# Searching 112 pair sums instead of 256, five searches placed in the query projection, and new prices in the up-projection's work list

## The chip, the cores and the metric

The kernel runs on one core of one Trainium2 chip. The metric is device time in microseconds (us) of one execution; three runs of the kernel before are given. Engine names are those of the profile: PE is TensorE (matmul), PEld its weight loads, DVE VectorE, ACT ScalarE, POOL GpSimd, SP the engine that only issues DMAs.

## What is computed

The reference is a two-layer model on 512 tokens of width 1024. Each layer ends in a PEER feed-forward block, and the change touches only that block:

```python
q = (h @ q_w).reshape(T, PEER_HEADS, 2, PEER_HALF)
s = jnp.einsum('thcd,ckd->thck', q, sub_keys)
s1, i1 = lax.top_k(s[:, :, 0], 16)          # 16 best of 128, first half
s2, i2 = lax.top_k(s[:, :, 1], 16)          # 16 best of 128, second half
cand_s = (s1[..., :, None] + s2[..., None, :]).reshape(T, 8, 256)
cand_i = (i1[..., :, None] * 128 + i2[..., None, :]).reshape(T, 8, 256)
best_s, best_pos = lax.top_k(cand_s, 16)
idx = jnp.take_along_axis(cand_i, best_pos, axis=-1)
gate = jax.nn.softmax(best_s, axis=-1)
a = jnp.einsum('nd,nhkd->nhk', hb, u[ib])   # ib: idx
w = gb * jax.nn.gelu(a, approximate=False)  # gb: gate
out = jnp.einsum('nhk,nhkd->nd', w, v[ib])
```

For each token and each of 8 heads, the 16 best of 16384 experts are found by two searches among 128 and one among the 256 sums of their results. Both lists `s1` and `s2` come out sorted, from best to worst.

## The kernel before

Tokens lie in four tiles of 128, numbered `tt` = 0 to 3. In each layer `peer` has three stages.

**Query projection** (lines 949 to 980). Sixteen chunks `c`, each 24 matmuls of 128x512 (`lin`, `mm3`, lines 200 to 214: every product is taken in three parts, high times high, high times low, low times high). The function `score` of one chunk runs after the next chunk's matmuls: it multiplies by the sub-keys (L971) and ACT copies the scores out, tiles 0 and 3 to `early` (L976, three buffers), tiles 1 and 2 to `late` (L977, which the profile calls `gv`). Chunks 2h and 2h+1 give head h. Each `score` advances the generator `bg_topk` by one step, and `bg_topk` searches a head of tiles 0 and 3 as soon as both its chunks are there, so every second step only waits. In the same chunks, `napply` (c = 3 to 10) makes the normalised activations for the next stage: a DVE operation (L760) and a copy on ACT (L764).

**Up-projection** (lines 982 to 1003). 128 chunks `j`, each 24 matmuls of 128x384 (`hhi`, `hlo`) over tiles 1 to 3; ACT makes the high part of each weight chunk (`whi`, L169) and POOL the low part in four pieces (`wlo`, L172). Tile 0 goes another way: its 128 x 16 experts are fetched row by row, by indirect DMAs that POOL issues (L695; 1.17 a chunk, `URATE`), five row buffers, and DVE multiplies each row with the activations (L678). Beside this stage runs a list of work, made in `bg` (lines 912 to 947). Each chunk adds 2.65 (`BRATE`) to a credit, an item is taken while the credit is above zero, and each takes its price off (`work`, lines 184 to 190):

```python
T: (6.0, topk of one head of one tile)
D: (0.3, decode_g) (5.0, decode_i first) (5.0, decode_i second) (0.8, decode_e)
G: (1.5, onehot for 4 tokens; its matmuls, gmm, two items later)
```

T is a search, D turns a tile's 128 winning positions into expert numbers and gates (D(0) starts the row fetches), G builds two one-hot matrices on DVE (`early` L884, `og` L886) whose product on PE (L898) spreads the gates over the experts; there are 96 G, 32 for each of tiles 1 to 3. The matrix so made goes to memory (`G`) by an ACT DMA every fourth G. The list's order is written out by hand in lines 931 to 934. Once it has ended, `load_g` reads `G` back in three parts on SP, one a chunk.

**Down-projection** (lines 1013 to 1051). 128 chunks again; the gates read back from `G` are multiplied with the first product (`GA`), and DVE, not POOL, makes `wlo`.

The change touches `topk` (L794), `decode_g`, `decode_i`, `decode_e` (L816 to L874), `bg_topk` (L904) and `bg` (L912).

Of the kernel before, what the change touches and what calls it, by code (L numbers as in the profile page):

```python
# [11 lines left out]
F32 = _mybir.dt.float32  # L12
# [50 lines left out]
class Net:  # L63
# [90 lines left out]
    def next_w(self):  # L154
# [5 lines left out]
        while self.ndma < min(len(self.srcs), i + self.LA + 1) or self.nsplit < min(len(self.srcs), i + self.SA + 1):  # L160
# [479 lines left out]
    def peer(self, L):  # L640
        nc, t, tc = self.nc, self.t, self.tc
        mm = nc.tensor.matmul
        vt = nc.vector
# [103 lines left out]
        with ExitStack() as ctx:  # L747
            mp = ctx.enter_context(tc.tile_pool(name="pm", bufs=2, reuse_waits="tile"))
# [26 lines left out]
            best = hp.tile([P, NTT, HEADS, TOPK], F32, name="best")  # L775
            pos = hp.tile([P, NTT, HEADS, TOPK], U32, name="pos")
# [17 lines left out]
            def topk(jobs):  # L794
                v = {}
                one, two = [], []
                for n, (tt, hd) in enumerate(jobs):
                    v[n] = mp.tile([P, 2, TOPK], F32, name=f"tv{n}")
                    for c in range(2):
                        src = early[hd][:, first.index(tt), c] if tt in first else late[:, later.index(tt), hd, c]  # L800
                        one.append((src, v[n][:, c, :], idx[:, c, tt, hd, :]))
                top16(one)
                for n, (tt, hd) in enumerate(jobs):
                    cand = mp.tile([P, TOPK, TOPK], F32, name=f"cand{n}", bufs=1)
                    vt.tensor_tensor(cand, v[n][:, 0, :, None].to_broadcast([P, TOPK, TOPK]),
                                     v[n][:, 1, None, :].to_broadcast([P, TOPK, TOPK]), op=OP.add)
                    two.append((cand.rearrange("p a b -> p (a b)"), best[:, tt, hd, :], pos[:, tt, hd, :]))
                top16(two)

            HK = HEADS * TOPK  # L810
            dec = {}
# [4 lines left out]
            def decode_g(tt):  # L816
                gt = mp.tile([P, HEADS, TOPK], F32, name="gt", bufs=1)
                vt.tensor_tensor(gt, best[:, tt], best[:, tt, :, 0:1].to_broadcast([P, HEADS, TOPK]), op=OP.subtract)
                dec[tt] = gt, []
                return lambda: nc.scalar.activation(gt, gt, AF.Exp, scale=self.rv[:, tt:tt + 1])  # L820

            def decode_i(tt, c):
                pi = mp.tile([P, HEADS, TOPK], U32, name="pi", bufs=1)
                if c == 0:
                    vt.tensor_single_scalar(pi, pos[:, tt], 4, op=OP.logical_shift_right)
                else:
                    vt.tensor_single_scalar(pi, pos[:, tt], 15, op=OP.bitwise_and)
                pb = mp.tile([P, TOPK, HEADS], F16, name="pb", bufs=1)
                vt.tensor_copy(pb, pi.rearrange("p h k -> p k h"))
                ib = mp.tile([P, TOPK, HEADS], F16, name="ib")  # L830
                vt.tensor_copy(ib, idx[:, c, tt].rearrange("p h a -> p a h"))
                eq = mp.tile([P, TOPK, HK], F16, name="eq", bufs=1)
                vt.tensor_tensor(eq.rearrange("p a (n q) -> p a n q", q=QT),  # L833
                                 fl(pb).rearrange("p (n q) -> p n q", q=QT)[:, None].to_broadcast([P, TOPK, HK // QT, QT]),
                                 i16[:, :, None, :].to_broadcast([P, TOPK, HK // QT, QT]), op=OP.is_equal)
                e4 = eq.rearrange("p a (k h) -> p a k h", h=HEADS)
                vt.tensor_tensor(e4, e4, ib[:, :, None, :].to_broadcast([P, TOPK, TOPK, HEADS]), op=OP.mult)  # L837
                n = TOPK // 2
                while n > 1:
                    vt.tensor_tensor(eq[:, :n], eq[:, :n], eq[:, n:2 * n], op=OP.add)  # L840
                    n //= 2
                f = mp.tile([P, HK], F32, name=f"fi{c}", bufs=1)
                vt.tensor_tensor(f, eq[:, 0], eq[:, 1], op=OP.add)
                dec[tt][1].append(f)

            def decode_e(tt):
                gt, fi = dec.pop(tt)
                sm = mp.tile([P, 2, HEADS], F32, name="sm")
                vt.tensor_reduce(sm[:, 0], gt, axis=AX.X, op=OP.add)
                vt.reciprocal(sm[:, 1], sm[:, 0])  # L850
                gk = mp.tile([P, TOPK, HEADS], F32, name="gk", bufs=1)
                vt.tensor_tensor(gk, gt.rearrange("p h k -> p k h"), sm[:, 1, None, :].to_broadcast([P, TOPK, HEADS]),
                                 op=OP.mult)
                if tt == 0:
                    ef = wg[:, 0]
                    vt.tensor_scalar(ef, fi[0], float(P), float(L * NBLK * P), op0=OP.mult, op1=OP.add)
                    vt.tensor_tensor(ef, ef, fi[1], op=OP.add)
                    vt.tensor_copy(eg, ef)
                    vt.tensor_copy(gate, fl(gk))

                def turn():
                    if tt == 0:
                        self.gi = 0
# [40 lines left out]
            def bg_topk():  # L904
                done = 0
                for hd in range(HEADS):
                    while self.hready <= hd:
                        yield
                    topk([(tt, hd) for tt in first])
                    yield  # L910

            def bg():  # L912
                items = []

                def T(tt, *hds):
                    for hd in hds:
                        items.append((6.0, lambda hd=hd: topk([(tt, hd)])))

                def D(tt):
                    items.append((0.3, lambda: decode_g(tt), 2))  # L920
                    items.append((5.0, lambda: decode_i(tt, 0)))
                    items.append((5.0, lambda: decode_i(tt, 1)))
                    items.append((0.8, lambda: decode_e(tt), 2))

                def G_(tt, lo, hi):
                    def one(b):
                        o = onehot(b)
                        return lambda: gmm(b, o)
                    for b in range(32 * tt + lo, 32 * tt + hi):
                        items.append((1.5, lambda b=b: one(b), 2))  # L930
                D(0), T(1, 0, 1), D(3), T(1, 2, 3, 4), G_(3, 0, 12), T(1, 5, 6), G_(3, 12, 20), T(1, 7), D(1)
                G_(3, 20, 28), T(2, 0), G_(3, 28, 32), T(2, 1), G_(1, 0, 4), T(2, 2), G_(1, 4, 8), T(2, 3)
                G_(1, 8, 12), T(2, 4), G_(1, 12, 16), T(2, 5), G_(1, 16, 20), T(2, 6), G_(1, 20, 22), T(2, 7), D(2)
                G_(1, 22, 32), G_(2, 0, 32)
                prev = []
                for cost, f, *late in items:
                    g = f()
                    for q in prev:
                        q[0] -= 1
                    while prev and prev[0][0] <= 0:  # L940
                        prev.pop(0)[1]()
                    if g is not None:
                        prev.append([late[0] if late else 1, g])
                    yield cost
                yield 3.0
                for _, g in prev:
                    g()
# [58 lines left out]
        with vctx:  # L1006
            mp = vctx.enter_context(tc.tile_pool(name="pv", bufs=3, reuse_waits="tile"))
# [5 lines left out]
            for j in range(NBLK):  # L1013
# [14 lines left out]
                w = self.next_w()  # L1028
# [528 lines left out]
```

## Time and profile before

| | us |
|---|---|
| median of three runs | 3432.62 (3429.08 to 3437.0) |
| profiled execution, its own time | 3430.42 |
| its span, first to last instruction | 3428.5 |
| PE busy | 3281.8 (96%) |
| DVE busy | 2712.8 (79%) |
| POOL busy | 1968.1 (57%) |
| ACT busy | 1452.7 (42%) |
| mean granted TensorE clock | 0.988 of full speed |

Busy shares are means over stages with different limits. PE's share hardly tells them apart, since matmuls overlap: what counts is how far apart successive matmuls start. The stages of the first layer's `peer` lie at 528 to 634 us (query), 634 to 1263 (up) and 1263 to 1803 (down); those of the second at 2080 to 2186, 2186 to 2816 and 2816 to 3356.

### The profile page before, as it was taken

Reading aid. Unit: us, or ns where it says so; the run is one execution under the profiler, and the core shown is the slowest. Engines: PE = TensorE matmul, PEld = TensorE weight load, DVE = VectorE, ACT = ScalarE, POOL = GpSimd, SP = SyncE. Lnnn points to the kernel's source line nnn. Section 1 sums busy time; section 2 is a strip of 40 time slices with the busy share of each in tenths; the row PEclk is TensorE's granted clock in tenths of the full one; section 3 lists DMA queues with packets and bytes.
Section 4 is the critical chain, followed back from the end, with each engine's and each line's share of the span. In section 5 each row is a group of like instructions: output and inputs, shape, how many; then the busy total and the mean of one; then the engine's idle time right before and its main releaser. Section 6 shows DMA issues by size and latency. Waiting matters only on the chain.

```text
span 3428.5 us, 52077 instructions
## 1 busy us (share of the span) xinstructions
PE 3281.8 (96%) x18814; PEld 3007.1 (88%) x18814; DVE 2712.8 (79%) x4880; ACT 1452.7 (42%) x2198; POOL 1968.1 (57%) x2168
## 2 busy tenths in 40 slices
PE   8999999998999999999998999999999999999997
PEld 5777777988999989999996668989998989999996
DVE  7667667899999748877877855899999837877775
ACT  4333334444545533333334553444445533333334
POOL 5444546799989884222216226689999994322214
PEclk9999999999999999999999999999999999999998
DMA  3222212488999989999983112488898989999982
GB/s 123 88 75 68 74 62 76 148 293 304 318 319 318 338 312 353 359 338 342 340 276 105 44 56 88 128 291 306 314 336 297 340 308 362 355 334 346 338 300 84
DMA packets 357298, 827.48 MB, mean 241 GB/s; under 512 B 30000, under 2 KB 196528, under 8 KB 350896
## 3 DMA queue, kind: packets, MB, share of 16 engines
q1 hardware_dynamic: 235136, 448.59, 40.4%
q0 software_dynamic: 73728, 268.47, 21.4%
q10 hardware_dynamic: 48176, 107.10, 8.1%
q8 instruction: 147, 2.41, 0.3%
q14 instruction: 111, 0.91, 0.1%
HBM read 717.09 MB, written 106.95 MB: 240 GB/s over the span
## 4 chain that ended last, share of the span: by engine, by line
PE 54%; DVE 32%; POOL 5%; DMA 4%; issue 3%; ACT 1%; POOLq 0%; SPq 0%; ACTq 0%; DVEq 0%
PE bank L202 16%; PE bank L203 16%; PE bank L204 16%; DVE row L678 6%; DVE early L884 6%; DVE og L886 5%; POOL wlo L172 4%; DMA row<-u,eg 2%; DVE eq L840 1%; POOL row L695 1%; DMA wraw<-v 1%; PE bank L971 1%; DVE eq L837 1%; DVE eq L833 1%; DMA wraw<-ut 1%
## 5 line engine op out<-in xcount | busy, mean ns | idle before, releaser
L172 POOL TENSOR_TENSOR wlo<-wraw,whi 128x256 fp32r<-128x256 f32 x1564 | 1279.4, 850 | 517.3 <-ACT whi L169 468.3
L169 ACT ACTIVATE whi<-wraw 128x1024 fp32r<-128x1024 f32 x647 | 685.6, 1061 | 787.8 <-issue 341.1
L695 POOL DMA_INDIRECT row<-v,eg x256 | 305.4, 1193 | 723.2 <-DVE yg L687 708.7
L204 PE MATMUL bank<-hhi,wlo 128*128 128x384 f32 x2048 | 695.1, 339 | 19.1 <-POOL wlo L172 18.7
L202 PE MATMUL bank<-hhi,whi 128*128 128x384 f32 x2048 | 703.6, 344 | 0.0
L203 PE MATMUL bank<-hlo,whi 128*128 128x384 f32 x2048 | 691.2, 338 | 0.0
L203 PE MATMUL bank<-vlo,whi 128*128 128x384 f32 x2032 | 684.6, 337 | 6.5 <-DVE vlo L744 6.5
L202 PE MATMUL bank<-vhi,whi 128*128 128x384 f32 x2032 | 685.4, 337 | 0.1
L204 PE MATMUL bank<-vhi,wlo 128*128 128x384 f32 x2032 | 684.3, 337 | 0.1
L172 DVE TENSOR_TENSOR wlo<-wraw,whi 128x1024 fp32r<-128x1024 f32 x256 | 313.4, 1224 | 159.4 <-ACT whi L169 158.3
L204 PEld LDWEIGHTS bank<-hhi,wlo 128*128 128x128 f32 x2048 | 387.4, 189 | 29.8 <-POOL wlo L172 29.4
L203 PEld LDWEIGHTS bank<-vlo,whi 128*128 128x128 f32 x2032 | 383.1, 189 | 8.0 <-DVE vlo L744 8.0
L202 PEld LDWEIGHTS bank<-hhi,whi 128*128 128x128 f32 x2048 | 388.4, 190 | 0.5 <-ACT whi L169 0.4
L203 PEld LDWEIGHTS bank<-hlo,whi 128*128 128x128 f32 x2048 | 388.3, 190 | 0.0
L202 PEld LDWEIGHTS bank<-vhi,whi 128*128 128x128 f32 x2032 | 383.0, 188 | 1.0 <-ACT vhi L742 0.4
L204 PEld LDWEIGHTS bank<-vhi,wlo 128*128 128x128 f32 x2032 | 383.0, 189 | 0.7 <-POOL wlo L172 0.7
L678 DVE SCALAR_TENSOR_TENSOR row<-row,pair 128x1024 f32<-128x1024 f32 x256 | 305.2, 1212 | 72.6 <-DMA row<-u,eg 72.3
L687 DVE SCALAR_TENSOR_TENSOR yg<-row,wg,yg 128x1024 f32<-128x1024 f32 x254 | 328.2, 1292 | 36.6 <-DMA row<-v,eg 36.5
L202 PE MATMUL bank<-z,whi 128*128 128x512 f32 x728 | 321.2, 441 | 3.4 <-DVE sg L1137 3.4
L695 POOL DMA_INDIRECT row<-u,eg x256 | 274.0, 1070 | 52.9 <-issue 30.3
L203 PE MATMUL bank<-z,whi 128*128 128x512 f32 x728 | 289.8, 398 | 4.6 <-DVE z L262 4.6
L204 PE MATMUL bank<-z,wlo 128*128 128x512 f32 x728 | 290.1, 399 | 0.0
(322 smaller groups left out, 4742.7 us busy)
## 6 DMA issues: line engine op xcount, KB each, us to landing
wraw<-ut SPq DMA_DIRECT2D x256, 512.0 KB, 4.7
wraw<-v SPq DMA_DIRECT2D x256, 512.0 KB, 6.1
wraw<-wlin SPq DMA_DIRECT2D x135, 512.0 KB, 3.5
GA<-ga ACTq DMA_DIRECT2D x256, 192.0 KB, 4.5
G<-gsz ACTq DMA_DIRECT2D x48, 1024.0 KB, 7.1
gv<-G SPq DMA_DIRECT2D x96, 512.0 KB, 9.5
gsz<-GA SPq DMA_DIRECT2D x256, 192.0 KB, 6.5
PJ<-nf ACTq DMA_DIRECT2D x16, 256.0 KB, 2.0
```

The costliest lines, as they stand in the source:

```text
L169: nc.scalar.activation(hi, r, AF.Copy)
L172: self.lo_eng.tensor_tensor(lo[:, q:q + n], r[:, q:q + n], hi.bitcast(F32)[:, q:q + n], op=OP.subtract)
L202: mm(out, whi, xhi, start=start, stop=False)
L203: mm(out, whi, xlo, start=False, stop=False)
L204: mm(out, wlo, xhi, start=False, stop=stop)
L678: vt.scalar_tensor_tensor(r, r, 1.0, self.pair, op0=OP.mult, op1=OP.mult, accum_out=wg[:, 0, j:j + 1])
L687: vt.scalar_tensor_tensor(yg, r, wg[:, 0, j:j + 1], yg, op0=OP.mult, op1=OP.add)
L695: nc.gpsimd.indirect_dma_start(out=got[i], out_offset=None, in_=t["u"] if i < NJ else t["v"].rearrange("a p d -> (a p) d"), in_offset=bass ...
L833: vt.tensor_tensor(eq.rearrange("p a (n q) -> p a n q", q=QT), fl(pb).rearrange("p (n q) -> p n q", q=QT)[:, None].to_broadcast([P, TOPK, ...
L837: vt.tensor_tensor(e4, e4, ib[:, :, None, :].to_broadcast([P, TOPK, TOPK, HEADS]), op=OP.mult)
L884: vt.tensor_tensor(pairs(o), iota.rearrange("p (a d) -> p a d", d=2)[:, None, None].to_broadcast([P, QT, 2, P // 2, 2]), alike(iT), op=OP. ...
L886: vt.tensor_tensor(pairs(og), pairs(o)[:, :, 0:1].to_broadcast([P, QT, 2, P // 2, 2]), alike(gT), op=OP.mult)
```

## The change

Three things are altered.

1. **Pair sums.** Instead of all 256 sums, 112 are made: the four best of the first list with all 16 of the second (64), and the other 12 with the four best of the second (48). With both lists sorted, the 16 best sums are among these. One addition of 256 becomes two, of 64 and 48, and the five search operations run over 112 elements. `decode_i` must now find the two list places from a position in the 112: with a constant shift more and `scalar_tensor_tensor` forms, three operations a half where there were two.
2. **Five searches.** Heads 0 to 4 of tile 1 leave the up-projection's list and go into `bg_topk`'s idle steps, after heads 2 to 6 of tiles 0 and 3.
3. **The list.** T is priced 5.2 (was 6.0), each half of D 6.2 (was 5.0), G 2.2 (was 1.5). Its order begins D(0), D(3), T(1, heads 5 and 6) instead of D(0), T(1, heads 0 and 1), D(3), T(1, heads 2 to 4). `BRATE` stays 2.65.

```diff
+QEARLY = 5
@@ topk
-                    cand = mp.tile([P, TOPK, TOPK], F32, name=f"cand{n}", bufs=1)
-                    vt.tensor_tensor(cand, v[n][:, 0, :, None].to_broadcast([P, TOPK, TOPK]),
-                                     v[n][:, 1, None, :].to_broadcast([P, TOPK, TOPK]), op=OP.add)
-                    two.append((cand.rearrange("p a b -> p (a b)"), best[:, tt, hd, :], pos[:, tt, hd, :]))
+                    cand = mp.tile([P, 4 * TOPK + 4 * (TOPK - 4)], F32, name=f"cand{n}", bufs=1)
+                    for a, m, w in ((0, 4, TOPK), (4, TOPK - 4, 4)):
+                        o = cand[:, TOPK * a:TOPK * a + m * w].rearrange("p (a b) -> p a b", b=w)
+                        vt.tensor_tensor(o, v[n][:, 0, a:a + m, None].to_broadcast([P, m, w]),
+                                         v[n][:, 1, None, :w].to_broadcast([P, m, w]), op=OP.add)
+                    two.append((cand, best[:, tt, hd, :], pos[:, tt, hd, :]))
@@ decode_i
+                pb = mp.tile([P, TOPK, HEADS], F16, name=f"pb{c}", bufs=1)
                 if c == 0:
+                    pk = mp.tile([P, HEADS, TOPK], U32, name="pk", bufs=1)
                     vt.tensor_single_scalar(pi, pos[:, tt], 4, op=OP.logical_shift_right)
+                    vt.tensor_single_scalar(pk, pos[:, tt], 2, op=OP.logical_shift_right)
+                    vt.scalar_tensor_tensor(pb, turned(pk), -12.0, turned(pi), op0=OP.add, op1=OP.max)
                 else:
-                    vt.tensor_single_scalar(pi, pos[:, tt], 15, op=OP.bitwise_and)
-                pb = mp.tile([P, TOPK, HEADS], F16, name="pb", bufs=1)
-                vt.tensor_copy(pb, pi.rearrange("p h k -> p k h"))
+                    vt.tensor_scalar(pm, pa, 4.0, 48.0, op0=OP.mult, op1=OP.add)
+                    vt.scalar_tensor_tensor(pm, pa, 16.0, pm, op0=OP.mult, op1=OP.min)
+                    vt.tensor_tensor(pb, turned(pos[:, tt]), pm, op=OP.subtract)
@@ bg_topk
                     topk([(tt, hd) for tt in first])
                     yield
+                    if 2 <= hd < 2 + QEARLY:
+                        topk([(1, hd - 2)])
+                        yield
@@ bg
-                        items.append((6.0, lambda hd=hd: topk([(tt, hd)])))
+                        items.append((5.2, lambda hd=hd: topk([(tt, hd)])))
-                    items.append((5.0, lambda: decode_i(tt, 0)))
-                    items.append((5.0, lambda: decode_i(tt, 1)))
+                    items.append((6.2, lambda: decode_i(tt, 0)))
+                    items.append((6.2, lambda: decode_i(tt, 1)))
-                        items.append((1.5, lambda b=b: one(b), 2))
-                D(0), T(1, 0, 1), D(3), T(1, 2, 3, 4), G_(3, 0, 12), T(1, 5, 6), G_(3, 12, 20), T(1, 7), D(1)
+                        items.append((2.2, lambda b=b: one(b), 2))
+                D(0), D(3), T(1, 5, 6), G_(3, 0, 12), T(1, 7), G_(3, 12, 20), D(1)
```

The order of the instructions moves in three places that matter. First DVE in the query projection, behind the search of head 2 of tiles 0 and 3 (`pos` are the winners' positions, `nf` the activations of `napply`, `early` and `gv` the scores). Before:

```order
L790 MAX_INDEX pos<-best,cand_5149 128x8
L790 MAX_INDEX pos<-best,cand_5151 128x8
L760 SCALAR_TENSOR_TENSOR nf<-x_97,cols,rs 128x384
L760 SCALAR_TENSOR_TENSOR nf<-x_99,cols,rs 128x384
L786 MAX tv_5264<-early 128x8 x2
```

and now:

```order
L761 SCALAR_TENSOR_TENSOR nf<-x_97,cols,rs 128x384
L787 MAX tv_5220<-gv_4681 128x8 x2
L788 MAX_INDEX idx<-tv_5220,gv_4681 128x8 x2
L789 MATCH_REPLACE gv_4681<-tv_5220,gv_4681 128x128 x2
L790 MAX tv_5220<-gv_4681 128x8 x2
L791 MAX_INDEX idx<-tv_5220,gv_4681 128x8 x2
L808 TENSOR_TENSOR cand_5231<-tv_5220 128x64
L808 TENSOR_TENSOR cand_5231<-tv_5220 128x48
L787 MAX best<-cand_5231 128x8
L788 MAX_INDEX pos<-best,cand_5231 128x8
L789 MATCH_REPLACE cand_5231<-best,cand_5231 128x112
L790 MAX best<-cand_5231 128x8
```

A whole search of tile 1 stands between the two `napply` operations that stood side by side; its last index search and the second `nf` follow.

Second, DVE early in the up-projection, from the last operation of D(0) on (`gate` is its result, `gt` the first operation of the next decode). Before:

```order
L859 COPY gate<-gk 128x128
L786 MAX tv_6013<-gv_4681 128x8 x2
L787 MAX_INDEX idx<-tv_6013,gv_4681 128x8 x2
L788 MATCH_REPLACE gv_4681<-tv_6013,gv_4681 128x128 x2
L789 MAX tv_6013<-gv_4681 128x8 x2
```

and now:

```order
L870 COPY gate<-gk 128x128
L821 TENSOR_TENSOR gt<-best 128x128
L831 TENSOR_SCALAR pi<-pos 128x128
L832 TENSOR_SCALAR pk<-pos 128x128
L833 SCALAR_TENSOR_TENSOR pb_6167<-pk,pi 128x128
```

The two searches that came here are gone, and D(3) follows D(0) at once, with the extra shift.

Third, SP at the end of the up-projection (`wraw<-ut` are its weight chunks, `wraw<-v` those of the down-projection, `gv<-G` the three parts read back). Before:

```order
L150 DMA wraw<-ut 128x1024 x113
L714 DMA gv_4681<-G_4673 128x8x128
L150 DMA wraw<-ut 128x1024
L714 DMA gv_4681<-G_4673 128x8x128
L150 DMA wraw<-ut 128x1024
L714 DMA gv_4681<-G_4673 128x8x128
L150 DMA wraw<-ut 128x1024 x13
L150 DMA wraw<-v 128x1024 x2
```

and now:

```order
L151 DMA wraw<-ut 128x1024 x127
L715 DMA gv_4681<-G_4673 128x8x128
L151 DMA wraw<-ut 128x1024
L715 DMA gv_4681<-G_4673 128x8x128
L151 DMA wraw<-v 128x1024
L715 DMA gv_4681<-G_4673 128x8x128
L151 DMA wraw<-v 128x1024
L723 DMA gsz<-GA_4674 128x384
```

The read-back stood 14 weight chunks earlier; now it lies right ahead of the down-projection's first chunks.

## Rows read from the trace of the kernel before

**Rows 1.** Busy time by engine in three stretches of layer 1 (windows view).

```profile
core 0: us, PE busy (x) PEld busy (x) DVE busy (x) ACT busy (x) POOL busy (x), PEclk, DMA share, GB/s
575.00:634.00 59.00, 59.00 (x291) 48.53 (x291) 46.42 (x239) 21.27 (x51) 35.05 (x46) 1.00 0.27 82
634.00:1176.00 542.00, 513.92 (x3400) 498.72 (x3399) 527.59 (x996) 275.75 (x348) 487.64 (x549) 0.98 0.87 301
1176.00:1263.00 87.00, 82.42 (x467) 79.01 (x464) 30.54 (x40) 31.09 (x43) 78.91 (x96) 1.00 0.91 318
```

**Rows 2.** Up-projection's matmuls by tile `hhi`, each layer: durations, first and last start.

```profile
L202 PE MATMUL bank<-hhi,whi x1024: 332/336/668, 634.1 to 1262.2; 128*128 128x384 f32 x171
...
L202 PE MATMUL bank<-hhi,whi x1024: 332/336/669, 2186.3 to 2815.8; 128*128 128x384 f32 x171
```

**Rows 3.** PE's waits, 634 to 1263: us in total, times, longest.

```profile
PE bank L898 <- DVE og L886: 19.6, 14, 3.5
PE bank L204 <- POOL wlo L172: 7.8, 9, 2.4
```

**Rows 4.** DVE by line, 634 to 1263: busy us, mean ns, idle before.

```profile
L678 DVE SCALAR_TENSOR_TENSOR row<-row,pair 128x1024 f32<-128x1024 f32 x128 | 152.6, 1212 | 35.6 <-DMA row<-u,eg 35.5
L884 DVE TENSOR_TENSOR early<-iota,iT 128x1024 f16<-128x1024 f16 x96 | 123.5, 1286 | 0.9 <-PE bank L898 0.9
L886 DVE TENSOR_TENSOR og<-early,gT 128x1024 f16<-128x1024 f16 x96 | 105.8, 1102 | 3.3
...
L831 DVE CAST ib<-idx 128x128 f16<-128x128 uint32 x8 | 5.5, 687 | 0.0
```

**Rows 5.** All operations on tile `eq` (four decodes), 634 to 1263: DVE busy.

```profile
634.00:1263.00 629.00, 51.75 (x48) 0.99 0.87 304
```

**Rows 6.** DVE timeline: one search alone, its first operation and what follows it.

```profile
709.13 0.48 DVE L786 MAX8 tv<-gv 128x8 f32<-128x128 f32 x2
...
714.32 0.40 DVE L873 SCALAR_TENSOR_TENSOR gT<-bank,gT 128x256 f16<-128x256 f32 x1
```

**Rows 7.** PE timeline inside one up-projection chunk and across one G.

```profile
1103.00 0.34 PE L203 MATMUL bank<-hlo,whi 128*128 128x384 f32 x1
...
1106.82 0.34 PE L204 MATMUL bank<-hhi,wlo 128*128 128x384 f32 x1
1107.00 0.62 PE L898 MATMUL bank<-og,early 128*128 128x128 f16 x8
...
1107.68 0.34 PE L203 MATMUL bank<-hlo,whi 128*128 128x384 f32 x1
```

**Rows 8.** POOL by line, 634 to 1263: busy us, mean ns, idle before.

```profile
L172 POOL TENSOR_TENSOR wlo<-wraw,whi 128x256 fp32r<-128x256 f32 x505 | 417.4, 858 | 34.2 <-ACT whi L169 32.1
L695 POOL DMA_INDIRECT row<-u,eg x128 | 138.3, 1080 | 27.3 <-issue 15.5 <-DVE row L678 4.4 <-DVE wg L682 2.5
```

**Rows 9.** Tile `wlo`, 634 to 1263: duration in ns, least, median, most.

```profile
L172 POOL TENSOR_TENSOR wlo<-wraw,whi x505: 712/744/1795, 636.6 to 1262.6; 128x256 fp32r<-128x256 f32 x169
```

**Rows 10.** DVE timeline in the query projection: one period of two searches together.

```profile
575.78 0.68 DVE L786 MAX8 tv<-early 128x8 f32<-128x128 f32 x3 [2.16 <-ACT early L976]
...
580.27 1.34 DVE L805 TENSOR_TENSOR cand<-tv 128x256 f32<-128x256 f32 x2
581.53 0.74 DVE L786 MAX8 best<-cand 128x8 f32<-128x256 f32 x2
...
585.21 1.12 DVE L760 SCALAR_TENSOR_TENSOR nf<-x,cols,rs 128x384 f32<-128x384 f32 x2
...
589.02 0.68 DVE L786 MAX8 tv<-early 128x8 f32<-128x128 f32 x3 [2.16 <-ACT early L976]
```

**Rows 11.** ACT's waits, 575 to 634: us in total, times, longest.

```profile
ACT hhi L764 <- DVE nf L760: 16.4, 2, 8.2
```

**Rows 12.** The page's DMA issues: count, size, median us from issue to landing.

```profile
G<-gsz ACTq DMA_DIRECT2D x48, 1024.0 KB, 7.1
gv<-G SPq DMA_DIRECT2D x96, 512.0 KB, 9.5
```

More of the change, by code (lines that the diff above doesn't have):

```diff
@@ L818, in decode_g @@
                 vt.tensor_tensor(gt, best[:, tt], best[:, tt, :, 0:1].to_broadcast([P, HEADS, TOPK]), op=OP.subtract)
-                dec[tt] = gt, []
+                dec[tt] = gt, [], []
                 return lambda: nc.scalar.activation(gt, gt, AF.Exp, scale=self.rv[:, tt:tt + 1])
@@ L823, in decode_i @@
                 pi = mp.tile([P, HEADS, TOPK], U32, name="pi", bufs=1)
+                pb = mp.tile([P, TOPK, HEADS], F16, name=f"pb{c}", bufs=1)
+                turned = lambda x: x.rearrange("p h k -> p k h")
                 if c == 0:
+                    pk = mp.tile([P, HEADS, TOPK], U32, name="pk", bufs=1)
                     vt.tensor_single_scalar(pi, pos[:, tt], 4, op=OP.logical_shift_right)
-                else:
-                    vt.tensor_single_scalar(pi, pos[:, tt], 15, op=OP.bitwise_and)
-                pb = mp.tile([P, TOPK, HEADS], F16, name="pb", bufs=1)
-                vt.tensor_copy(pb, pi.rearrange("p h k -> p k h"))
+                    vt.tensor_single_scalar(pk, pos[:, tt], 2, op=OP.logical_shift_right)
+                    vt.scalar_tensor_tensor(pb, turned(pk), -12.0, turned(pi), op0=OP.add, op1=OP.max)
+                    dec[tt][2].append(pb)
+                else:
+                    pa, pm = dec[tt][2][0], pi.bitcast(F32).rearrange("p h k -> p (h k)").rearrange(
+                        "p (k h) -> p k h", h=HEADS)
+                    vt.tensor_scalar(pm, pa, 4.0, 48.0, op0=OP.mult, op1=OP.add)
+                    vt.scalar_tensor_tensor(pm, pa, 16.0, pm, op0=OP.mult, op1=OP.min)
+                    vt.tensor_tensor(pb, turned(pos[:, tt]), pm, op=OP.subtract)
                 ib = mp.tile([P, TOPK, HEADS], F16, name="ib")
@@ L846, in decode_e @@
             def decode_e(tt):
-                gt, fi = dec.pop(tt)
+                gt, fi, _ = dec.pop(tt)
                 sm = mp.tile([P, 2, HEADS], F32, name="sm")
```

## The prediction

> **What bounds the kernel now.** I read the windows view first, since the page's shares are means over unlike stages. In the query projection PE is busy all 59.0 of 59 us, and DVE 46.4: a fifth of DVE is free there [rows 1]. In the up-projection it is the other way round. From 634 to 1176 DVE is busy 527.6 of 542 us, and in the 87 us after that only 30.5: its list has ended, at chunk 108 of 128 [rows 1]. So for 108 chunks DVE sets the pace, then it idles. The stage takes 628.1 us from its first to its last matmul, 629.5 in the second layer [rows 2].
>
> What PE loses by that stands in its waits: 19.6 us for the one-hot products `og`, 7.8 for `wlo` [rows 3]. The second is DVE's too in part: a late row multiplication holds a row buffer, POOL waits for it in order, and the `wlo` behind it comes late. The granted clock is 0.98 over the stretch, against 1.00 in the query projection [rows 1]: that costs up to 11 us more.
>
> How far could the stage shrink? Three floors, worked out the same way.
>
> - PE. Inside a chunk, 22 matmuls start in 3.82 us, 0.1736 apart [rows 7]; 24 make 4.17. One G adds 0.86 - 2 x 0.1736 = 0.51 (from L204 at 1106.82 to L203 at 1107.68, two steps without it) [rows 7]. 128 x 4.17 + 96 x 0.51 = **583 us**.
> - POOL. 417.4 for `wlo`, 138.3 for the rows of u, 12 for some 11 rows of v at 1.08, and 15.5 of "issue" ahead of the row fetches [rows 8]: 583. In the first 8 chunks there are no rows, and POOL can't work ahead of its buffers: it has 4 x 0.858 = 3.43 of 4.17 to do [rows 7, 8], so 6 are lost. **589 us.**
> - DVE, next, since this is what the change alters.
>
> **The change, part by part.**
>
> *A search over 112.* In a pair of searches, four searches of 128 take 580.27 - 575.78 = 4.49, 1.12 each; two of 256 take 585.21 - 581.53 = 3.68, 1.84 each [rows 10]. The difference is 0.72 for 128 elements; 0.72 / 128 = 5.6 ns each, so 112 instead of 256 saves 144 x 5.6 = 0.81. The two small additions replace one of at least 0.4 (the pair's took 1.26 [rows 10], with POOL in the way); bounds: they save 0.2, or cost 0.2 more. I take nothing. A search alone goes from 714.32 - 709.13 = 5.19 [rows 6] to 4.38, a pair from 9.43 [rows 10] to 7.8.
>
> *A decode.* 51.75 / 4 = 12.9 on `eq` [rows 5], and some six casts, shifts and products of at most 0.69 each (L831 [rows 4]): 12.9 to 17.0; I take 17. One operation more in each half, at most 0.69: 18.4 at most, 17.3 if they take 0.15. I take 18.4.
>
> *The five searches in the query projection.* A period of two chunks is 589.02 - 575.78 = 13.24 [rows 10], which PE sets. DVE would have 7.8 (pair) + 4.38 (tile 1) + 1.12 (`napply`, twice) [rows 10] = 13.3. It fits, barely. ACT stands in between: its `hhi` waits 8.2 us a period for `nf` behind the pair [rows 11], and now waits a second time, behind the new search. The pair after that can then start up to 1 us late, in the three periods that still have `napply`; after that 12.2 against 13.24. ACT's copies for PE are due a chunk (6.6 us) later, so I cost it at nothing. Cover gone, it is what DVE overruns: 0.1 to 1 us for three periods, 3 a layer.
>
> *DVE's part of the up-projection.* A G costs 1.286 + 1.102 = 2.39, a row 1.21 [rows 4]. Before: 16 searches (8 heads of tiles 1 and 2) x 5.19 = 83; 4 decodes x 17 = 68; 96 x 2.39 = 229; rows from chunk 7 to 108, 101 x 1.17 x 1.21 = 143. Sum 523, and DVE was busy 527.6 [rows 1]: the prices hold. PE would have needed 108 x 4.17 + 49 = 499. Now: 11 x 4.38 = 48; 4 x 18.4 = 74; 229; rows over 122 chunks, 115 x 1.17 x 1.21 = 163. Sum **514**, over 122 chunks in which PE needs 122 x 4.17 + 49 = 558.
>
> That is the second half of the gain, and the greater: the list's prices. All old ones sum to 284, which 2.65 a chunk pays off by chunk 108; the new ones to 322, by chunk 122. G was priced 1.5 against 2.39, so in a row of G DVE got 2.65 / 1.5 x 2.39 + 1.42 = 5.6 us a chunk while PE took 4.17 + 1.77 x 0.51 = 5.1; now 2.65 / 2.2 x 2.39 + 1.42 = 4.3 against 4.8. A decode is still under its price (18.4 against 13.5): each throws DVE back by about 5 us, twice in a row at the start, and the chunks of T and G after it make that good at 0.4 to 0.5 a chunk. That no search stands between D(0) and D(3) costs nothing; the row fetches start one chunk earlier.
>
> So DVE's floor falls below PE's, and **POOL is next**, at 589. The binding engine before lost 542 - 528 = 14 to its neighbours [rows 1]; I add 13 to POOL's 589: 602. That is 26 less in the first layer and 27 in the second: **-53**. Why POOL's need should stay is in the trace: a `wlo` takes 712 to 1795 ns, median 744, mean 858 [rows 9, 8], though all are alike. What lengthens them is DVE's work beside them, and the 96 G and 4 decodes remain, only spread.
>
> [...]
>
> *The end of the list.* It now ends 14 chunks later, 5 chunks (21 us) ahead of the down-projection. Behind the last G come its matmuls and ACT's copy, 1 us, the write of `G`, 7.1, the read, 9.5 [rows 12], and three short steps for the first product, about 2: 20 of 21 us. SP stands still for the write, and the first down-projection weights queue behind it. Between 0 and 8 a layer; I take 3, as two of three transfers overlap: **+6**.
>
> The down-projection, attention and the rest hold nothing of the change.
>
> Sum: -53 + 6 = -47 on the profiled execution's 3430.4, which is 2.2 under the median: 3383, or **3385** against the median.
>
> **The rivals.**
>
> - *PE alone bounds* (0.18). POOL's long `wlo` come from DVE being always busy, and go with it: 512 x 0.744 = 381 instead of 439 [rows 9, 8] puts POOL at 531, below PE. The stage becomes 583, saving 45 and 46: 3432.6 - 91 + 6 = 3348. For it: medians near the least. Against: contention belongs to operations, and none is gone.
> - *Little gain* (0.15). DVE at 514 of 558 with items of 6 us and POOL at 589 jam each other, and the stage stays within 10 of its length: 3412 to 3430.
> - *Slower* (0.08). One mechanism: the read-back of `G`. DVE comes to the list's end late, by what decodes and prices leave over; then write and read (7.1 + 9.5 [rows 12]) lie open ahead of the first product, 17 a layer, 33 in all, and the stage gains under 8 a layer: 3433 - 16 + 33 = 3450. It decides if DVE is over 9 us late (2% of 514) at chunk 122. For it: 20 of 21 us. Against: 0.4 us a chunk of slack in the last 35 chunks, which are all G.
> - *It does not do what it says* (0.06): the searches' gain is small, the pace no different, and everything falls within 7 us of the median.
>
> **How the numbers follow.** My forecast, POOL-bound, has 0.53; its own range is 3365 to 3410. About 0.2% (7 us) is what a measurement of this kernel tells from no change. Faster: 0.53 + 0.18 + 0.13 of the third = 0.84; within: 0.06 + 0.02 = 0.08; slower 0.08. The range goes from PE's floor, 3346, up to 3426, which leaves out the last two cases and a little at each end.
>
> **What would show it.** Right: DVE's busy share in the up-projection falls from 97% to under 90% and is even until chunk 122; `og` waits fall from 19.6 us below 6; the stage measures 595 to 610 us; POOL's busy share there is over 94%; the query projection stays within 2 us; FIND_INDEX8 over 112 takes about 0.26 us. Wrong: PE waits for ACT's `ga` or `whi` in the query projection (the searches don't fit); `og` waits as long as before (prices still too low); PE idle over 10 us at the first down-projection chunks (read-back); a stage under 590 (no POOL bound).

## The result, and the profile after

The changed kernel takes 3388.67 us (median of four runs, 3385.17 to 3394.31); the kernel before took 3432.32 beside it. The ratio is 0.9881, 95% interval 0.9868 to 0.9893: 44 us faster, against a forecast of 47 (3385). The profiled execution has a span of 3392.5 against 3428.5, 36 less. The total came out close. The terms behind it did not all, and the cause that I gave for the largest of them is only half of the truth.

The three stretches of [rows 1], moved to the new stage's times:

```profile
577.00:636.00 59.00, 58.35 (x288) 48.26 (x287) 54.97 (x327) 22.02 (x51) 33.83 (x45) 1.00 0.25 81
638.00:1180.00 542.00, 531.36 (x3425) 513.24 (x3425) 489.89 (x923) 276.27 (x347) 500.49 (x572) 0.99 0.88 308
1180.00:1251.00 71.00, 66.97 (x436) 63.27 (x436) 52.95 (x45) 32.43 (x40) 67.95 (x73) 1.00 0.97 345
```

In the query projection DVE now works 55.0 of 59 us instead of 46.4: the five searches. In the next 542 us it works 489.9 where it worked 527.6, and PE is busy 17 us more. Only behind that does DVE's list end.

The up-projection's matmuls by tile `hhi`, one view for each layer, against [rows 2]:

```profile
L203 PE MATMUL bank<-hhi,whi x1024: 332/338/667, 638.1 to 1250.7; 128*128 128x384 f32 x171
...
L203 PE MATMUL bank<-hhi,whi x1024: 332/338/522, 2170.2 to 2778.2; 128*128 128x384 f32 x171
```

The stage takes 612.6 and 608.0 us instead of 628.1 and 629.5. PE's waits in it, against [rows 3], then POOL and DVE by line, against [rows 8] and [rows 4]:

```profile
PE bank L205 <- POOL wlo L173: 10.0, 12, 3.1
PE bank L878 <- DVE gk L863: 2.3, 1, 2.3
PE bank L909 <- DVE og L897: 2.0, 2, 1.8
```

```profile
L173 POOL TENSOR_TENSOR wlo<-wraw,whi 128x256 fp32r<-128x256 f32 x504 | 413.5, 853 | 16.8 <-ACT whi L170 14.6
L696 POOL DMA_INDIRECT row<-u,eg x128 | 141.3, 1104 | 26.7 <-issue 15.3 <-DVE row L679 3.9 <-DVE eg L869 1.3
L696 POOL DMA_INDIRECT row<-v,eg x12 | 13.8, 1148 | 2.2 <-issue 1.9 <-DVE wg L683 0.2
...
L895 DVE TENSOR_TENSOR early<-iota,iT 128x1024 f16<-128x1024 f16 x96 | 128.6, 1340 | 1.6 <-PE bank L909 1.6
L897 DVE TENSOR_TENSOR og<-early,gT 128x1024 f16<-128x1024 f16 x96 | 97.0, 1010 | 3.3
L842 DVE CAST ib<-idx 128x128 f16<-128x128 uint32 x8 | 10.0, 1251 | 0.0
L788 DVE FIND_INDEX8 pos<-best,cand 128x8 uint32<-128x112 f32 x16 | 4.2, 269 | 0.0
```

All of these are rows of layer 1, 638 to 1251 us. The waits for `og` are down from 19.6 to 2.0 us; those for POOL's `wlo` are not, 10.0 against 7.8. A `wlo` takes 853 ns on the mean as before (858).

**Where the 36 us are.** From the first and last starts of the tiles `sk`, `hlo` and `vhi` I cut each profiled execution of this study into stages. "Up" runs from the first to the last `hlo` start, "down" from there to the last `vhi` matmul's end. The stretches ahead of the two query projections hold nothing that any run here changes. Yet they take 539 to 546 us (548.6 once) and 285 to 290, each by itself and with no relation to the edit. So I compare stages, and medians only beside them. One execution of each kernel is profiled, and its two layers differ in "up" by up to 13 us (b3_split): a difference of a few us in that column tells something only where the medians go the same way.

| kernel | query, layers 1, 2 | up | down | median, ratio to before |
|---|---|---|---|---|
| before | 94.0, 94.0 | 628.0, 629.4 | 540.7, 540.1 | |
| after | 93.9, 93.9 | 612.6, 607.9 | 540.6, 543.2 | 0.9881 |
| a1_prices | 94.1, 94.1 | 603.2, 611.6 | 544.8, 540.6 | 0.9896 |
| a2_sums | 93.0, 92.9 | 625.1, 634.4 | 539.6, 539.3 | 0.9979 |
| a3_five | 99.4, 100.2 | 644.6, 641.0 | 539.2, 540.8 | 1.0116 |
| a4_oldprices | 93.9, 93.9 | 627.9, 639.5 | 541.4, 540.9 | 1.0037 |
| b1_lo34 | 93.9, 93.9 | 589.7, 589.6 | 543.2, 543.0 | 0.9769 |
| c1_halfrow | 93.9, 93.9 | 608.7, 612.7 | 541.3, 543.6 | 0.9902 |
| b2_true | 93.9, 93.9 | 604.1, 596.3 | 541.1, 542.0 | 0.9855 |
| b3_split | 93.9, 93.9 | 610.2, 597.4 | 540.8, 543.2 | 0.9879 |
| c3_order | 93.9, 93.9 | 600.8, 604.1 | 541.9, 543.6 | 0.9837 |
| d1_both | 93.9, 93.9 | 603.4, 601.6 | 541.6, 544.7 | 0.9842 |
| c2_lop2 | 93.7, 93.7 | 615.7, 611.4 | 540.5, 541.0 | 0.9934 |
| b4_rate28 | 93.9, 93.9 | 618.6, 617.1 | 539.6, 540.7 | 0.9934 |

The gain is the up-projection's: 15.4 and 21.5, 36.9 in all. The down-projection gives 3.0 back.

To see where in the stage, I take the start of each chunk's first `hlo` matmul, and from each period between two of them 4.17 and 0.51 for each G in it ([rows 7]; PE's floor in the prediction). What is left is PE's loss in that chunk:

| loss in us, layers 1, 2 | chunks 8 to 23: D(0), D(3) | 32 to 47: D(1) | 72 to 95: D(2) | all other | sum |
|---|---|---|---|---|---|
| before | 8.6, 8.6 | 13.5, 12.3 | 8.8, 12.3 | 13.2, 11.8 | 44.1, 45.0 |
| after | 8.5, 10.5 | 7.1, 3.1 | 2.4, 4.4 | 11.5, 6.6 | 29.5, 24.6 |
| b1_lo34 | 2.8, 2.6 | 0.9, 0.9 | 0.9, 0.9 | 2.9, 3.0 | 7.5, 7.4 |
| c1_halfrow | 7.3, 7.1 | 4.6, 2.7 | 6.8, 10.4 | 6.3, 9.8 | 25.0, 30.0 |
| c3_order | 1.4, 1.4 | 5.8, 8.0 | 7.8, 5.5 | 3.5, 5.4 | 18.5, 20.3 |

So PE's loss is no tax on every chunk: in the changed kernel 103 and 107 of the 127 periods lose under 0.1 us, and 18.0 of the 29.5 and 18.0 of the 24.6 us lie in the three columns of the decodes. The largest of the three is behind D(0) and D(3), and there the change gained nothing.

**One such place**, layer 1 of the changed kernel, in the timeline: DVE, then POOL, then PE.

```profile
674.18 0.22 DVE L870 COPY gate<-gk 128x128 f32<-128x128 f32 x1
...
675.21 3.50 DVE L842 CAST ib<-idx 128x128 f16<-128x128 uint32 x1
...
695.70 0.47 DVE L863 TENSOR_TENSOR gk<-gt,sm 128x128 f32<-128x128 f32 x1
696.09 1.21 DVE L679 SCALAR_TENSOR_TENSOR row<-row,pair 128x1024 f32<-128x1024 f32 x1
...
701.58 1.20 DVE L679 SCALAR_TENSOR_TENSOR row<-row,pair 128x1024 f32<-128x1024 f32 x1
...
695.88 2.95 POOL L173 TENSOR_TENSOR wlo<-wraw,whi 128x256 fp32r<-128x256 f32 x4
698.99 0.95 POOL L696 DMA_INDIRECT row<-u,eg  x1 [0.16 <-DVE tv L790]
703.06 0.94 POOL L696 DMA_INDIRECT row<-u,eg  x1 [3.12 <-DVE row L679]
704.01 2.79 POOL L173 TENSOR_TENSOR wlo<-wraw,whi 128x256 fp32r<-128x256 f32 x4
...
704.80 0.69 PE L205 MATMUL bank<-hhi,wlo 128*128 128x384 f32 x1 [3.05 <-POOL wlo L173]
```

`gate` is D(0)'s last result and sends off the first row fetch. D(3) then holds DVE from 674.3 to 696.1, 21.8 us, one cast alone 3.50 (it ends, at 678.7, with four `wlo` that POOL runs from 675.75 to 678.56). Its price is 13.5, so the list is soon in credit again: DVE multiplies one row, then does a search of 4.3 us, and only then three more rows. The five row buffers are full meanwhile: POOL stands 3.12 us ahead of a row fetch with the `wlo` of the next chunk queued behind it, and PE waits 3.05 us for that `wlo`.

### The profile page after: what moved, and what is told of

Its sections match the earlier page's. It is cut to its first block, busy times and chain, and to the rows that moved or that the text cites. A ratio compares the mean times of both kernels' runs of the same rounds, so it can differ in the third digit from the quotient of the medians.

```text
span 3392.5 us, 52158 instructions
## 1 busy us (share of the span) xinstructions
PE 3284.1 (97%) x18814; PEld 3010.0 (89%) x18814; DVE 2695.9 (79%) x4960; ACT 1462.5 (43%) x2198; POOL 1996.4 (59%) x2168
## 3 DMA queue, kind: packets, MB, share of 16 engines
q0 software_dynamic: 73728, 268.47, 21.5%
## 4 chain that ended last, share of the span: by engine, by line
PE 56%; DVE 19%; POOL 12%; DMA 7%; issue 5%; ACT 1%; SPq 0%; POOLq 0%; ACTq 0%; DVEq 0%
PE bank L203 17%; PE bank L204 17%; PE bank L205 17%; POOL wlo L173 8%; DMA row<-u,eg 5%; POOL row L696 3%; DVE row L679 2%; DVE early L895 1%; DVE eq L851 1%; DVE og L897 1%; DVE cand L808 1%; DMA wraw<-v 1%; DVE idx L788 1%; DVE idx L791 1%; PE bank L543 1%
## 5 line engine op out<-in xcount | busy, mean ns | idle before, releaser
L173 POOL TENSOR_TENSOR wlo<-wraw,whi 128x256 fp32r<-128x256 f32 x1564 | 1261.2, 839 | 489.2 <-ACT whi L170 460.4
L696 POOL DMA_INDIRECT row<-v,eg x256 | 343.0, 1340 | 678.2 <-DVE yg L688 665.6
L173 DVE TENSOR_TENSOR wlo<-wraw,whi 128x1024 fp32r<-128x1024 f32 x256 | 313.1, 1223 | 119.9 <-ACT whi L170 118.8
L696 POOL DMA_INDIRECT row<-u,eg x256 | 283.8, 1109 | 54.1 <-issue 30.5
```

What stands on the lines that cost most here:

```text
L173: self.lo_eng.tensor_tensor(lo[:, q:q + n], r[:, q:q + n], hi.bitcast(F32)[:, q:q + n], op=OP.subtract)
L696: nc.gpsimd.indirect_dma_start(out=got[i], out_offset=None, in_=t["u"] if i < NJ else t["v"].rearrange("a p d -> (a p) d"), in_offset=bass ...
```

## The experiments

### The change in parts

**a1_prices**, against the kernel before (shortened):

```diff
-URATE, VRATE, BRATE = 1.17, 0.94, 2.65
+URATE, VRATE, BRATE = 1.17, 0.94, 2.85
-T 6.0, half of D 5.0, G 1.5
+T 5.2, half of D 6.2, G 2.2
```

> The kernel before with the new prices alone (T 5.2, half of D 6.2, G 2.2). All 16 searches stay in the list, over 256 sums, and their prices sum to 351; so that the list still ends at chunk 123 and not in the drain ahead of the end, BRATE is 2.85 here. Theory 1 (pace): the gain comes from G no longer being packed tighter than DVE can make them; DVE's demand is 543 of the 558 us that PE needs for 122 chunks, so this run holds two thirds or more of the whole gain of 44: 3395 to 3408, and og waits fall from 19.6 to below 6 us a layer. Theory 2 (work): the gain comes from the 29 us a layer that leave DVE's part of this stage (searches and shorter sums); then prices alone give little, 3420 or more.

Measured: 3395.38 us, ratio 0.9896 [0.9882, 0.9911], the up-projection 21.3 us a layer shorter on the mean. The `og` waits are a little above what theory 1 set:

```profile
PE bank L898 <- DVE og L886: 8.0, 6, 2.4
PE bank L204 <- POOL wlo L172: 4.3, 7, 1.4
PE bank L867 <- DVE gk L852: 2.8, 1, 2.8
```

Theory 1 holds in the main: the prices, with `BRATE` at 2.85, bring as much as the full change does in this stage (18.5 a layer), with all 16 searches still in the list and over 256 sums. Which of the three prices does it was not tried.

**a2_sums**: `cand` of 112 and the new `decode_i` alone, in the kernel before.

> The kernel before with the 112 sums alone (search and decode), old prices, all 16 searches in the list. Theory 1 (pace): 16 x 0.8 = 13 us less DVE work and up to 6 more in the decodes, but in a list packed too tight in its G rows; DVE still sets those: at most 7 us a layer, 3418 to 3432. Theory 2 (work): DVE sets the pace until chunk 108, so each us that it no longer works there is a us of the stage: 13 less 6, twice, 3418; at the upper end both agree, so the og waits decide: as before (over 15) by theory 1.

Measured: 3425.79 us, 0.9979 [0.9968, 0.9990]. The stage keeps its length (629.8 on the mean against 628.7); the query projection is 1.0 shorter. The time is theory 1's, but its sign failed in one layer of two: `og` waits fell to 9.4 us in the first, whose stage is 2.9 shorter, and to 16.7 from 22.4 in the second, whose stage is 5.0 longer. So `og` waits alone don't tell the length of this stage.

**a3_five**: `bg_topk` and the list's order of the changed kernel, with 256 sums and the old prices.

> The kernel before with the five searches of tile 1 in the query projection alone: 256 sums, old prices, the new order of the list. Search pair and single search now need 9.4 + 5.2 + 1.1 = 15.7 of 13.2 us in the periods with napply and 14.6 in the others, so DVE overruns there by 1.4 to 2.5 in each of five periods: the query projection grows by up to 9 us a layer unless idle steps take it up. In the up-projection 26 us of DVE work go; theory 1 (pace): the list (sum 254) ends at chunk 96, its G rows as tight as before, og waits stay over 15: no gain beyond 8 us a layer, 3425 to 3445. Theory 2 (work): 26 less a layer against 0 to 9 in the query projection: 3380 to 3400.

Measured: 3468.12 us, 1.0116 [1.0099, 1.0132]: slower by more than either theory allowed. The query projection grows by 5.4 and 6.2 us, as expected. PE waits for ACT there, since DVE no longer fits in:

```profile
577.00:636.00 59.00, 55.20 (x263) 45.45 (x262) 57.31 (x282) 18.86 (x44) 31.98 (x41) 0.97 0.26 81
...
PE bank L975 <- ACT ga L970: 4.3, 2, 3.8
...
PE bank L899 <- DVE og L887: 28.8, 18, 3.1
```

The up-projection grows too, by 16.6 and 11.6, although 26 us of DVE work left it: `og` waits rise to 28.8, and 13.0 and 13.7 us are lost in chunks 8 to 23, behind the two decodes that now stand side by side. Theory 2 is out. The short sums are what lets the five searches fit: a4_oldprices, which differs from this run by the sums and their decode alone, keeps 93.9 there.

**a4_oldprices**: the changed kernel with 6.0, 5.0 and 1.5.

> The changed kernel with the old prices (6.0, 5.0, 1.5), everything else of the change kept. Its list sums to 254 and ends at chunk 96. DVE's demand until there is 48 + 74 + 229 + 128 for rows = 479 us, in which PE would need 449: DVE sets the pace to chunk 96. Theory 1 (pace): 479 + 14 of coupling + 32 chunks at 4.35 = 632, as long as before: 3425 to 3437, og waits over 12. Theory 2 (work): 35 to 40 us less DVE work a layer than before, at most 5 of it lost to pace: 3390 or less.

Measured: 3441.96 us, 1.0037 [1.0023, 1.0050], 5 us above theory 1's range, and `og` waits of 10.7 where it set over 12; theory 2 is far off. The changed list without the prices is a loss: 14.7 and 16.8 us go in chunks 8 to 23 alone. Less DVE work buys nothing here at the old prices.

### What the stage waits for: POOL's slack or DVE's

**b1_lo34**, in the changed kernel's up-projection (shortened; the last chunks keep all four pieces):

```diff
-for q in range(0, D, n):
+for q in range(0, D - n, n):
     self.lo_eng.tensor_tensor(lo[:, q:q + n], r[:, q:q + n], ...
-third product of k = 6, 7: wlo, xhi
+third product of k = 6, 7: whi, xhi
```

> The changed kernel with a quarter of POOL's work on wlo left out in the up-projection: three pieces of 256 columns instead of four, and the products of the last quarter with the low part use the high part instead, so that PE's work is the same and the low part of that quarter is missing from the result. POOL's need falls by 0.85 x 120 = 100 us a layer, far below PE's 583. Theory POOL (the prediction's): POOL's 589 + 13 is what bounds the stage; it falls to PE's 583 or close, 15 to 25 us a layer: 3340 to 3360. Theory bursts: PE sets the pace in all chunks but those beside the decodes and at the list's end, which stay; POOL only hands a late row on: 0 to 8 us a layer, 3372 to 3389.

Measured: 3352.08 us, 0.9769 [0.9756, 0.9782]; the stage 22.9 and 18.3 us shorter, 7.5 over PE's floor. That is theory POOL's time. Windows from the first to the last `hlo` (changed kernel 638 to 1251: DVE 542.84, POOL 568.44), and POOL's waits behind D(3):

```profile
638.00:1228.00 590.00, 588.79 (x3859) 575.15 (x3859) 460.73 (x970) 303.23 (x386) 462.48 (x522) 1.00 0.92 323
...
POOL row L699 <- DVE row L682: 3.8, 1, 3.8
```

But DVE was relieved too, by 82 us, and D(3) took 18.5 us instead of 21.8, so the run alone does not say whose slack counts. The waits speak for POOL's: behind D(3) DVE again does one row, a search and then three rows, and POOL stands 3.8 us for its row, more than the 3.12 above. Yet PE waits for no `wlo` at all. POOL was far enough ahead: it idles 94 us for `whi` in this stage, against 14.6 in the changed kernel. Behind D(1) and D(2), part of the gain may be the shorter decodes.

**c1_halfrow** takes DVE's part by itself:

```diff
-vt.scalar_tensor_tensor(r, r, 1.0, self.pair, ...
+vt.scalar_tensor_tensor(r[:, :512], r[:, :512], 1.0, self.pair[:, :512], ...
```

> The changed kernel with half of each row multiplication of tile 0 left out (512 of 1024 columns; the sums of tile 0 miss that half): DVE's work falls by about 128 x 0.55 = 70 us a layer, evenly over the stage, as much as its busy time fell in the run with three quarters of wlo (541.5 to 468.5 in 605 us); POOL issues and computes what it did. Theory POOL: what that run gained came from POOL's own 100 us; here POOL's need stays at 566 + 15, so at most 4 us a layer, by wlo less held up beside shorter rows: 3380 to 3389. Theory DVE: what that run gained came from DVE's 73 us of relief, and POOL has slack enough: 15 to 20 us a layer here too: 3348 to 3362.

Measured: 3398.16 us, 0.9902 [0.9887, 0.9917]. The stage takes 608.7 and 612.7: on the mean it is 0.4 us longer than the changed kernel's. The window, and PE's waits up to 1238 us:

```profile
640.00:1249.00 609.00, 597.83 (x3857) 574.25 (x3855) 483.26 (x965) 308.30 (x387) 566.99 (x645) 1.00 0.89 313
...
PE bank L205 <- POOL wlo L173: 7.4, 12, 2.0
```

DVE has 60 us less to do and POOL the same: nothing gained. DVE's total is not what limits. D(3) takes 21.8 us as before, and most of the loss behind it stays, 7.3 and 7.1 us in chunks 8 to 23. Theory DVE is out. The median lies 9 us above theory POOL's range as well; the stage, 0.9 us longer in all, does not show why.

**c2_lop2**, in the kernel b2_true (below), asks whether POOL's need alone is enough:

```diff
-LOP = 4
+LOP = 2
```

> The kernel with true prices (T 4.4, half of D 9.1, G 2.0) and wlo in two pieces of 512 columns instead of four of 256. If POOL limits and each piece has a fixed part of 0.06 us or more, POOL's need falls by 256 x 0.06 = 15 us a layer or more and 5 to 10 of them are gained: 3357 to 3367. If the time goes by elements alone, or longer pieces hold DVE up for longer: 3375 to 3390.

Measured: 3407.03 us, 0.9934 [0.9920, 0.9948], slower than both expectations, 11.6 and 15.1 us a layer longer than b2_true, although POOL's `wlo` work fell by some 60 us (both views up to 1238 us):

```profile
L173 POOL TENSOR_TENSOR wlo<-wraw,whi 128x512 fp32r<-128x512 f32 x248 | 346.0, 1419 | 73.7 <-ACT whi L170 72.0
...
PE bank L909 <- DVE og L897: 10.1, 3, 4.8
PE bank L878 <- DVE gk L863: 4.7, 1, 4.7
PE bank L205 <- POOL wlo L173: 2.3, 1, 2.3
```

Now POOL idles 72 us for `whi` and DVE is late: the decodes' operations on `eq` take 63.0 us instead of 50.3. That a longer `wlo` piece holds DVE up for longer is my reading of it; `early`, 1252 ns on the mean against 1340 in the changed kernel, does not show it. So POOL's slack does not decide by itself: here DVE's decodes grew as it did.

### The decodes: price, size, place

**b2_true**: T 4.4, half of D 9.1, G 2.0 in the changed kernel.

> The changed kernel with the list's prices at the durations of its own trace: T 4.4, half of D 9.1, G 2.0 (2.35 less a part of PE's 0.51, which each G gives DVE as time), BRATE as it is; the list's sum is 321, so it ends at the same chunk, 121. Theory bursts: the chunks after D(0), D(3), D(1) and D(2) get the time to make good, but each half is still issued as one block of 9 us, so at most half of the 10 to 17 us of excess at the decodes goes: 3378 to 3388. Theory POOL: no change, 3385 to 3392.

Measured: 3376.9 us, 0.9855 [0.9839, 0.9870]; 8.5 and 11.6 us a layer gained in the profiled execution, which is the fastest of its four; the medians differ by 12. The loss in chunks 8 to 23 falls from 8.5 and 10.5 to 2.0 and 1.2, more than I had expected of a price.

**b3_split**: as b2_true, and each half of D in two items (the first half shown).

```diff
-items.append((9.1, lambda: decode_i(tt, 0)))
+items.append((4.1, lambda: decode_i(tt, 0)))
+items.append((5.0, lambda: decode_r(tt, 0)))
```

> As b2_true, with each half of D in two items, priced 4.1 (places, eq, ib) and 5.0 (products and sums), so that row multiplications come between them. Theory bursts: a row then waits 5 us at most instead of 9 and the row buffers (five, 3.6 us apart) bridge that; most of the 10 to 17 us of excess at the decodes goes: 3362 to 3375. Theory POOL: no change, 3385 to 3392.

Measured: 3387.07 us, 0.9879 [0.9864, 0.9894]: no gain over b2_true, rather a loss (the stage 6.1 and 1.1 us longer). So at these prices shorter items gain nothing more; at the change's own prices splitting was not tried. What the price changes is how soon the list goes on, ahead of the rows that wait: inside layer 1's D(3) DVE does no row in the changed kernel, four in b2_true and four here.

**c3_order**, prices of the change kept (three searches between D(0) and D(3), where the expectation says four; two behind D(3), as in the changed kernel):

```diff
-D(0), D(3), T(1, 5, 6), G_(3, 0, 12), T(1, 7), G_(3, 12, 20), D(1)
+D(0), T(1, 5, 6, 7), D(3), T(2, 0, 1), G_(3, 0, 12), G_(3, 12, 20), D(1)
-G_(3, 20, 28), T(2, 0), G_(3, 28, 32), T(2, 1), G_(1, 0, 4), ...
+G_(3, 20, 28), G_(3, 28, 32), G_(1, 0, 4), ...
```

> The changed kernel, its prices kept, with four searches between D(0) and D(3) and two behind D(3): the same items in all. The prediction's step (that no search stands between the two decodes costs nothing): no change, 3384 to 3393. Theory bursts: DVE comes out of D(0) some 6 us late (18.4 against a price of 12.4) and makes good 0.8 in each search priced 5.2 and done in 4.4, so of the 8.0 and 9.6 us of excess in chunks 8 to 15 a third to a half goes: 3378 to 3384.

Measured: 3373.34 us, 0.9837 [0.9824, 0.9851], the fastest kernel of the study that computes all of the model; the expectation of theory bursts was 3378 to 3384. The loss in chunks 8 to 23 falls to 1.4. Behind D(1) and D(2) it is not smaller (13.6 and 13.5 us together, against 9.5 and 7.5), in the rest it is (3.5 and 5.4, against 11.5 and 6.6). PE's waits up to 1238:

```profile
PE bank L205 <- POOL wlo L173: 3.4, 5, 1.4
PE bank L878 <- DVE gk L863: 3.2, 1, 3.2
PE bank L909 <- DVE og L897: 0.3, 1, 0.3
```

**d1_both**: c3_order's list with b2_true's prices.

> Both that helped: the changed kernel with searches between and behind D(0) and D(3), and the prices of the trace (T 4.4, half of D 9.1, G 2.0). Theory bursts: a late row blocks POOL, which has no slack to make it good; the order cleared chunks 8 to 23, the true prices most of what is left at D(1) and D(2) (4 to 8 us of 18 to 20 a layer): 3358 to 3370. If the two mend the same loss (both clear chunks 8 to 15, and G at 2.0 is packed 10% tighter than at 2.2): 3371 to 3380.

Measured: 3376.38 us, 0.9842 [0.9825, 0.9859], as fast as either alone: the two mend the same loss. In chunks 8 to 23 it is 2.0 and 1.2 us with the prices, 1.4 and 1.4 with the order, 1.5 and 1.3 with both. That the prices would save more at D(1) and D(2) did not come; why was not tried.

### The end of the list

**b4_rate28**: the changed kernel with BRATE 2.80.

> The changed kernel with BRATE 2.80 instead of 2.65: the list ends at chunk 115 instead of 122 and G is read back 30 us earlier. If the late read-back costs what PE loses between the start of chunk 127 and the first full down-projection chunk (16 to 18 us now, 11 in the kernel before), 5 to 7 us a layer come back, less up to 3 where G is packed 6% tighter: 3378 to 3386. If that loss only changed its place (in the kernel before, the first chunks of the down-projection lost 5 to 6 us that they do not lose now), the first chunks lose as much again: 3387 to 3394.

Measured: 3405.28 us, 0.9934 [0.9920, 0.9947], slower than both expectations. The first read of `G` is issued at 1198.7 instead of 1226.9, and the down-projection gains 1.0 and 2.5 us by it: that is all that an earlier read-back gives. The loss there mostly changes its place: from the start of chunk 127 to the first `vhi` matmul pass 15.7 and 17.8 us in the changed kernel, 11.9 and 10.5 here, 10.5 and 10.9 in the kernel before, but the next eight chunks lose 0.0 and 0.8, 1.5 and 4.7, 6.2 and 5.7. The up-projection loses 6.0 and 9.2, for a pace 6% faster. That was the price I had put at 3 at most.

## Why the prediction came out right, and where its steps failed

- **A search over 112: right.** A search alone takes 4.34 us (588.18 to 592.52 in layer 1's query projection) against 4.38, and FIND_INDEX8 over 112 takes 0.269. A pair takes 8.4 instead of 7.8 (from 579.24 to 587.66): its four small additions need 1.74 where two long ones took 1.26, 0.24 more for each search. Over all pairs of the query projection the four take from 0.49 to 2.59, so my bound of 0.2 either way was too narrow.
- **The five searches cost nothing: right.** The query projection takes 93.9 both times, against 94.0. PE waits once for ACT, 0.6 us. The cover was thin, as said: with 256 sums (a3_five) it is gone, and 5.4 to 6.2 a layer is paid.
- **A decode at 18.4 at most: failed for D(3).** D(0) took 18.2 to its `gk`, D(3) 21.8 and, in layer 2, 22.5. The step took 0.69 for a cast from [rows 4]; that is a mean, and in this place one `ib` took 3.50 and the three additions on `eq` 4.91 where D(0)'s took 2.75.
- **"That no search stands between D(0) and D(3) costs nothing": failed, and this is the largest error.** c3_order puts three there and gains 7.8 us a layer on the mean; in chunks 8 to 23 the loss falls by 7.1 and 9.1. Nor did the row fetches start earlier: 36.2 us into layer 1's stage, against 35.8. I had written that the chunks of T and G behind them would make the 5 us good at 0.4 to 0.5 a chunk; but the list does not wait for DVE, and POOL, stopped for rows meanwhile (3.12 us in the timeline), has nothing to make it good with.
- **DVE below PE, then POOL next at 589, coupling 13: half right.** POOL's need is 413.5 + 141.3 + 13.8 + 15.3 + 1.9 + 6 = 592, and b1_lo34 against c1_halfrow shows that its slack counts and DVE's total does not (what shorter decodes add in b1_lo34 stays open). But POOL does not pace the stage chunk by chunk, as the table of losses shows, and POOL is busy 568.4 of 613 us, 93%, not the 94 I had named. The 13 was a size carried over from another binding engine, with no row of its own; it measured 21 and 16. DVE's share up to 1180 us fell to 90.4%, just short of the sign I had set (under 90). So the term -53 came out as -37, and the first layer's 612.6 lies outside the 595 to 610 that I had set.
- **The end of the list, +6: measured +3.** More time passes ahead of the first product and less in the chunks behind it; b4_rate28 bears out that little of the read-back lies open.
- **The prices as the greater half of the gain: right, and more than that.** They bring as much as the whole change in this stage (a1_prices, with `BRATE` 2.85). The other two parts bring nothing there by themselves: without the prices the kernel takes 10 us more than before (a4_oldprices).
- **The rivals.** *PE alone bounds* rested on POOL's `wlo` becoming shorter; they stayed at 853 ns. *Little gain* and *slower* did not come; the read-back's price is bounded by b4_rate28.

Against the profiled execution the sum missed by 11 us (-36 for -47), against the medians by 4: the profiled execution of the changed kernel is the slowest of its four. The two terms come out as -34 instead of -47, so a median within 4 us of the forecast is luck in part. What stays open is the loss between the up- and the down-projection: "down" takes 539 to 545 us in every run, however early the list ends and whatever POOL has to do. What sets it was not tried.

## What to carry to other kernels

Price the items of a paced list by the durations in the trace: an underpriced item sends the engine on to the next one while its steady work waits, and here new prices were worth 36 of the 44 us. Put short items between two long ones: that gave another 15 us here. Before forecasting from a floor, look where the loss lies chunk by chunk: here POOL without slack passed a stop of 3.12 us on to PE as 3.05, and with slack hid one of 3.8.

## What the runs showed of the hardware that was not expected

DVE and POOL delay each other, and far from evenly over DVE's operations. In the changed kernel `early` takes 675 ns at best and 3590 at most; with a quarter of `wlo` gone its mean falls from 1340 to 851. A `wlo` takes 716 to 1795 ns in the same stage of the changed kernel, and the 35 of 504 with no DVE operation beside them 725 to 758.

```profile
L895 DVE TENSOR_TENSOR early<-iota,iT x96: 675/1179/3590, 711.9 to 1222.7; 128x1024 f16<-128x1024 f16 x96
...
L679 DVE SCALAR_TENSOR_TENSOR row<-row,pair x128: 1200/1214/1223, 696.1 to 1204.7; 128x1024 f32<-128x1024 f32 x128
...
L898 DVE TENSOR_TENSOR early<-iota,iT x96: 677/742/2222, 706.7 to 1198.2; 128x1024 f16<-128x1024 f16 x96
```

The row multiplications beside the same `wlo` take 1200 to 1223 ns, each of the 128. And c1_halfrow, which halves them, leaves `wlo` at 850 ns. I had counted every DVE operation as a rival of `wlo`, which is how c1_halfrow came to be expected to shorten it. The cast `ib`, with an eighth of their elements, took from 0.26 to 3.50 us in the changed kernel. What decides which operations are held up no run here shows.

Cutting POOL's work into fewer pieces saves POOL time (1419 ns for 512 columns against twice 846) and costs DVE some: it is busy 563.9 of 600 us in c2_lop2 (638 to 1238) and 540.7 of 605 in b2_true (635 to 1240), and POOL 493.6 and 564.4. In c2_lop2 a small operation, the subtraction `pb` of 128 elements, took up to 3205 ns, against 725 in b2_true.
